# A decoder block on one core: chunk steps issued behind products, operands formed from PSUM, norm weights spread by matmuls

## The chip, the cores and the metric

The kernel runs on one core of a Trainium2 chip. The metric is the device time of one execution in microseconds, as a median over runs. TensorE (PE) multiplies, VectorE (DVE), ScalarE (ACT) and GpSimd (POOL) do the rest, and SyncE (SP) and ACT issue the DMAs. PSUM is the memory in which products arrive, SBUF the one for operands.

## The reference

One block of a hybrid decoder, all in float32: 1024 positions, model width 1024.

```python
u = rmsnorm(h, norm_mix_w)
gate_a, gate_s, b_a, c_a, v_a, z, xbc, dt_raw = split(u @ w_in)
y_a = (b_a * causal_dwconv(c_a * v_a, conv_a_w)) @ w_a_out        # short gated conv
xbc = silu(causal_dwconv(xbc, ssd_conv_w) + ssd_conv_b)           # width 4
y   = ssd_chunked_scan(xh, dt, a, bs, cs)    # 32 heads of 64, 4 groups, state 128, chunks of 128
y_s = gated_group_rmsnorm(y + d_skip * xh, z, ssd_norm_w) @ w_s_out
h   = h + (sigmoid(gate_a) * y_a + sigmoid(gate_s) * y_s) @ w_o
v   = rmsnorm(h, norm_ffn_w)
h   = h + conv_gated_mlp(v, w_up, ffn_conv_w, ffn_conv_b, w_down) # inner width 2816
return rmsnorm(h, final_norm_w)
```

Within a chunk of 128 positions the scan is a masked product with decays exp(a_cum[l] - a_cum[s]); between chunks a state per head is carried on.

## The kernel before, in words

Positions and inner dimensions are held as 128 partitions by 512 or 1024 columns. Every float32 product is made of three products of rounded parts: a value is split into hi (a cast on ACT, `split`, L148) and lo = value - hi (a subtraction on DVE or POOL, L149), and `product` (L268) adds hi x hi, hi x lo and lo x hi, 12 matmuls of 128x512 into one PSUM buffer.

The projections u @ W_in and v @ W_up use a scheme of the Strassen-Winograd kind: for two column blocks of weights and the two halves of positions and of the inner dimension, seven products take the place of eight. The operands of the activations are a11, a12 (first half of the positions, the two halves of the inner dimension), a22, s1, s2, s3, s4 (with a21 and a22 of the second half: s1 = a21 + a22, s2 = s1 - a11, s3 = a11 - a21, s4 = a12 - s2); those of the weights are b11, b21, b22 and the sums t1 to t4, which `Pair.operands` forms on POOL. `Pair` makes the seven products of a pair; sums so far (`m1`, `u2`, `u3`) are copied from PSUM by ACT (L311, L331) or added by DVE (L314, L333), and `done` hands a finished pair on. `then` interleaves the last products of a pair with the first of the next.

`rms_rows` (L174 to L179) normalises a tile of 128 positions: a square with its sum on ACT, a power on POOL, and one DVE instruction that multiplies by the row's factor and by the weights nw (L179), broadcast to all partitions by a DMA of 512 KB (L433, behind the first two x tiles). `fill_first` (L207) transposes a normalised tile of the first half on TensorE (`pt_u`), splits it into a11 and a12, and copies both from PSUM back over the tile. `fill_second` (L215) does the second half in three stages: s1 and a22 with an ACT copy of each PSUM tile (L233, L236), then s2 and s3 by DVE from those SBUF copies (L240, L242), then s4. For u the kept first half gives a11 and a12; for v, the FFN's input, POOL adds hi and lo again (L229). In names, u or v marks the operand: us4l is the lo part of u's s4.

The order: x is normalised and transposed; three gate pairs (`head`, names with g) start with their a11 and a12 products while the second half's operands are made; then come the dt columns, whose result `decays` turns into decays per head and position (a chain on DVE and ACT; 6 transposes `tkp`, L593, copied to the tile tk); then the pairs of BEFORE (xb: the conv's inputs, z) and BESIDE. From BESIDE on, a clock counts the products: after each, `tick` (L394) runs what is due. Each of 32 chunks (4 groups of 8) is a generator `ssd_chunk` whose stages are due at 17 + 6s + offset: LOAD_M and LOAD_IN -9 (DMAs on ACT's queue, L715, L718), DECAY -6 (8 relus and an exponential on ACT, L724, L725, to the mask tile m), TRANS -4 (transposes px, pb, product pc, L730 to L734; DVE multiplies m by pc, L752), LOAD_Z -3, DIAG 0 (products pd, po, pst, L770 to L783), SQUARES 3, NORM 6 (a column sum pn, L813, a power on POOL, L819, and each fourth chunk a transpose pr, L823). `conv4` (L604 to L617) makes four taps, a silu and the store of an xb tile.

Then follow the output products (`y_a`, `s_out`, `out_proj`), in whose shadow v is normalised (`v_norm`, L1000 to L1009) and v's operands filled, the up pairs (`ffn_pair`) and the down products.

A scheduler puts the instructions of each engine in order, from the order of the code and a model of their times; `tc.issue_after(i)` makes what is written in its block and runs on i's engine stand behind i. PSUM has four buffers for products (`mm`) and four for the rest (`sd`); c2 is a pool of 6 tiles of 512 columns, t2 one such tile.

Of the kernel before, what the change touches and what calls it, by code (L numbers as in the profile page):

```python
# [65 lines left out]
def tile_block(  # L66
# [147 lines left out]
    def fill_second(A, v, t, name, first=None, own=None):  # L214
# [8 lines left out]
        def whole(c, nm):  # L223

            if first is not None:
                return blocks(first[:, halves[c == "a12"]])
            hi, lo = (f32(a[:, :, ts]) for a in A[c])
            o = blocks(c2(f"{nm}{name}{t}"))
            pool.tensor_tensor(o, hi, lo, op=ALU.add)  # L229
            return o  # L230
# [2 lines left out]
        act.copy(s1, pts[1])  # L233
        dve.tensor_tensor(s1, s1, pts[0], op=ALU.add)
# [5 lines left out]
        dve.tensor_tensor(s1, s1, a11, op=ALU.subtract)  # L240
# [1 line left out]
        dve.tensor_tensor(a21, a11, a21, op=ALU.subtract)  # L242
# [3 lines left out]
        a12 = whole("a12", "a12")
        s4 = a12 if own is None else blocks(
            own.tile([P, HALF], F32, tag="own", name=f"own{name}{t}", bufs=4)
        )
        dve.tensor_tensor(s4, a12, s1, op=ALU.subtract)  # L250
        if first is not None:
# [9 lines left out]
    def product(ps, c, w, start=True, stop=True, held=False):  # L261


        hi, lo = (t.rearrange("p (k c) -> p k c", k=4) for t in w)
        n = 0
        for wt, ct in ((hi, c[0]), (hi, c[1]), (lo, c[0])):
            for k in range(4):
                pe.matmul(  # L268
                    ps, wt[:, k, :], ct[:, k, :],
                    start=(start and n == 0), stop=(stop and n == 11), skip_group_check=held,  # L270
                )
                n += 1

    class Pair:
# [27 lines left out]
        def first(self, late=False, hold=True, place=None):  # L302
# [8 lines left out]
            act.copy(self.m1, p)  # L311
# [16 lines left out]
        def so_far(self, o, c, w, nm):  # L328

            if self.hold:  # L330
                act.copy(o, self.prod(c, w, nm, self.u))  # L331
            else:
                dve.tensor_tensor(o, self.m1, self.prod(c, w, nm), op=ALU.add)  # L333
# [278 lines left out]
    def conv4(ci, t):  # L612
        cv = b4(f"cv{t}")
        taps(cv, ci, scw[:, t, :], scb[:, t : t + 1])
        act.activation(cv, cv, AF.Silu)
# [86 lines left out]
    def ssd_chunk(s):  # L702
# [116 lines left out]
        pool.tensor_tensor(r[:, c % 4 : c % 4 + 1], rs, nhalf, op=ALU.pow)  # L819
# [538 lines left out]
```

## Time and profile before

| | |
|---|---|
| median of 3 runs | 1973.09 us (1970.45 to 1977.09) |
| the profiled execution | 1974.46 us; its span 1972.7 us |
| busy: TensorE, DVE, ACT, POOL | 1914.5, 1289.6, 962.0, 1236.3 us |
| mean granted clock of TensorE | 0.989 of full speed |
| DMA | 338.42 MB, mean 172 GB/s |

The span is the time between the first and the last instruction of the profiled execution; 1.8 us lie around it. Busy time of one engine overlaps that of the others. The granted clock is the share of full speed that the throttle allows TensorE; a matmul under half the clock is busy for twice the time. A row of a group has the line in the kernel, engine, operation, output<-inputs, shape, count, then busy time and mean ns of one, then idle time of the engine ahead of it and what ended most of that. A row of a wait has the engine that waits, output and line of the waiting instruction, the releaser with its line, then total, count and longest.

### The profile page before, as it was taken

How to read it: one execution, taken by the hardware profiler on the slowest of the kernel's cores; microseconds unless marked ns; L12 is line 12 of the kernel's file. 1: busy time of each engine (PE TensorE's matmuls, PEld its weight loads, DVE VectorE, ACT ScalarE, POOL GpSimd, SP SyncE). 2: the span in 40 equal slices, each digit the busy share in tenths (PEclk: the TensorE clock that was granted, in tenths of full speed). 3: DMA queues.
4: the chain of work that ended last, by engine and by line, in shares of the span. 5: the costliest groups of instructions: out<-in, count | busy, mean ns of one | idle time of the engine just before them, and what ended most of it. 6: DMA issues, size and time to landing. Idle time of an engine off the chain costs nothing.

```text
span 1972.7 us, 25409 instructions
## 1 busy us (share of the span) xinstructions
PE 1914.5 (97%) x8986; PEld 1572.0 (80%) x8986; DVE 1289.6 (65%) x1429; ACT 962.0 (49%) x1636; POOL 1236.3 (63%) x915
## 2 busy tenths in 40 slices
PE   7899999999999999999999999998999999999998
PEld 6678887787788778888888888876888888878886
DVE  8655567767776777777664833479854655585555
ACT  6345457677546664443542323354344444453334
POOL 6657776866776776676445533458876787845342
PEclk9899999999999999999999999998999999999999
DMA  4133355545445554443998974451323344487653
GB/s 166 54 111 121 122 164 172 162 150 190 155 133 164 164 164 124 146 157 110 382 376 279 356 250 161 161 170 35 136 80 108 101 150 163 139 285 264 206 188 143
DMA packets 180175, 338.42 MB, mean 172 GB/s; under 512 B 15280, under 2 KB 87760, under 8 KB 179024
## 3 DMA queue, kind: packets, MB, share of 16 engines
q1 hardware_dynamic: 93264, 253.95, 37.7%
q10 hardware_dynamic: 86784, 82.85, 13.1%
q8 instruction: 70, 1.15, 0.2%
q14 instruction: 57, 0.47, 0.1%
HBM read 247.34 MB, written 89.41 MB: 171 GB/s over the span
## 4 chain that ended last, share of the span: by engine, by line
PE 80%; DVE 7%; ACT 4%; issue 3%; DMA 3%; POOL 2%; ACTq 1%; SPq 0%; POOLq 0%; DVEq 0%
PE pb11up L268 10%; PE so L268 9%; PE pt1up L268 6%; PE pb11xb L268 5%; PE ya L268 4%; PE pb11cv L268 4%; PE d L1151 3%; PE d L1153 3%; PE d L1152 3%; PE pb11z L268 3%; PE pb21up L268 3%; PE pb11ba L268 2%; PE pt1cv L268 2%; PE pt1xb L268 2%; DMA m<-acd 2%
## 5 line engine op out<-in xcount | busy, mean ns | idle before, releaser
L608 DVE SCALAR_TENSOR_TENSOR cv<-xbc,scw,cv 128x1024 f32<-128x1024 f32 x72 | 122.6, 1704 | 46.3 <-ACT cv L604 45.0
L608 DVE SCALAR_TENSOR_TENSOR h<-fci,fcw,h 128x1024 f32<-128x1024 f32 x44 | 85.9, 1953 | 74.1 <-ACT h L604 73.3
L724 ACT ACTIVATE m<-m,tk 128x128 f32<-128x128 f32 x256 | 79.1, 390 | 95.3 <-DMA m<-acd 91.4
L149 POOL TENSOR_TENSOR l_ws<-raw_ws,h_ws 128x512 fp32r<-128x512 f32 x32 | 46.3, 1447 | 71.1 <-PE so L268 40.8
L148 ACT CAST h_ws<-raw_ws 128x512 fp32r<-128x512 f32 x64 | 39.9, 623 | 96.8 <-PE so L268 69.3
L268 PE MATMUL so<-yh,h_ws 128*128 128x512 f32 x256 | 69.0, 391 | 0.0
L268 PE MATMUL so<-yl,h_ws 128*128 128x512 f32 x256 | 68.6, 389 | 0.0
L268 PE MATMUL so<-yh,l_ws 128*128 128x512 f32 x256 | 68.5, 389 | 0.0
L148 ACT CAST h_wo<-raw_wo 128x512 fp32r<-128x512 f32 x48 | 29.7, 621 | 60.3 <-PE wo L985 32.7
L808 DVE TENSOR_TENSOR eb<-eb 128x256 f32<-128x256 f32 x32 | 28.1, 879 | 45.6 <-ACT eb L806 45.6
L149 DVE TENSOR_TENSOR l_ws<-raw_ws,h_ws 128x512 fp32r<-128x512 f32 x32 | 25.1, 785 | 50.0 <-PE so L268 25.5
L149 POOL TENSOR_TENSOR l_wo<-raw_wo,h_wo 128x512 fp32r<-128x512 f32 x24 | 32.3, 1346 | 39.1 <-PE wo L985 30.7
L268 PEld LDWEIGHTS so<-yh,l_ws 128*128 128x128 f32 x256 | 48.0, 188 | 10.0
L268 PEld LDWEIGHTS so<-yl,h_ws 128*128 128x128 f32 x256 | 48.0, 188 | 10.0
L268 PEld LDWEIGHTS so<-yh,h_ws 128*128 128x128 f32 x256 | 47.8, 188 | 9.7
L1128 DVE TENSOR_TENSOR h<-h 128x1024 f32<-128x1024 f32 x22 | 48.7, 2212 | 9.8 <-ACT h L1127 9.6
L314 DVE TENSOR_TENSOR fci<-fci,pb21up 128x512 f32<-128x512 f32 x18 | 12.4, 688 | 60.3 <-PE pb21up L268 60.3
L149 POOL TENSOR_TENSOR l_t3up<-raw_2up,h_t3up 128x512 fp32r<-128x512 f32 x22 | 30.3, 1376 | 32.7 <-PE pb11up L268 32.7
L984 PE MATMUL wo<-l_wo,mh 128*128 128x512 f32 x128 | 50.0, 391 | 0.0
L983 PE MATMUL wo<-h_wo,mh 128*128 128x512 f32 x128 | 49.9, 391 | 0.0
L985 PE MATMUL wo<-h_wo,ml 128*128 128x512 f32 x128 | 49.7, 391 | 0.0
L1127 ACT ACTIVATE h<-h 128x1024 f32<-128x1024 f32 x22 | 23.4, 1062 | 52.7 <-DVE h L608 52.7
(1125 smaller groups left out, 6571.8 us busy)
## 6 DMA issues: line engine op xcount, KB each, us to landing
m<-acd ACTq DMA_DIRECT2D x32, 512.0 KB, 3.9
raw_ws<-in_w_s_out SPq DMA_DIRECT2D x32, 512.0 KB, 4.7
ssd_in<-cv ACTq DMA_DIRECT2D x24, 512.0 KB, 3.1
in<-ssd_in ACTq DMA_DIRECT2D x32, 384.0 KB, 3.8
raw_wo<-in_w_o SPq DMA_DIRECT2D x24, 512.0 KB, 3.8
wd<-in_w_down SPq DMA_DIRECT2D x22, 512.0 KB, 7.0
td<-wd SPq DMA_DIRECT2D x44, 256.0 KB, 4.3
raw_2up<-in_w_up SPq DMA_DIRECT2D x22, 512.0 KB, 3.4
```

Source lines behind the costliest of these rows:

```text
L148: act.copy(hi, v)
L149: (eng or pool).tensor_tensor(lo, v, f32(hi), op=ALU.subtract)
L268: pe.matmul(ps, wt[:, k, :], ct[:, k, :], start=(start and n == 0), stop=(stop and n == 11), skip_group_check=held,)
L608: dve.scalar_tensor_tensor(cv, ci[:, j : j + SEQ], w[:, j : j + 1], cv, op0=ALU.mult, op1=ALU.add)
L724: act.activation(m[:, h, :], m[:, h, :], AF.Relu, bias=a)
L983: pe.matmul(pss[t], mh, wh, start=k == 0, stop=False)
L984: pe.matmul(pss[t], mh, wl, start=False, stop=False)
L985: pe.matmul(pss[t], ml, wh, start=False, stop=k == NK - 1)
L1128: dve.tensor_tensor(cv, cv, h3, op=ALU.mult)
L1151: pe.matmul(ps, aa[0][:, ts], bb[0], start=k == 0, stop=False)
L1152: pe.matmul(ps, aa[0][:, ts], bb[1], start=False, stop=False)
L1153: pe.matmul(ps, aa[1][:, ts], bb[0], start=False, stop=k == KF - 1)
```

## The change

1. The norm weights nw come as one row of 4 KB (first on SP's queue); two f32 matmuls against a row of ones spread it over the partitions, and DVE copies it from PSUM.
2. `fill_first`: for u the lo part of a12 is made by POOL from the kept copy, and the kept copy of a11 by DVE instead of ACT. For v, a11 is now kept too (4 more ACT copies, a pool of its own).
3. `fill_second`: s3 and s2 are formed by DVE with one operand in PSUM; the ACT copy of a21 (8 of them) and POOL's new sum of a11 for v (4) are gone. For u, s4's split is a fourth stage, run within the first gate pair, behind the addition u2 of that pair on DVE.
4. The second gate pair's t2 gets a c2 buffer.
5. `decays` stops ahead of its transposes; these are written behind the third pair of BEFORE.
6. `tick`: what is due is issued behind the last matmul of the product (on TensorE) and behind the last copy of product sums (on ACT). conv4's silu and store come two products later. The transpose pr is a stage of its own, due at +8.

Instructions in all: PE 8528 to 8530, ACT 1838 to 1826, DVE 1431 to 1433, POOL and SP as before.

```diff
-STAGES = LOAD_M, LOAD_IN, DECAY, TRANS, LOAD_Z, DIAG, SQUARES, NORM = -9, -9, -6, -4, -3, 0, 3, 6
+STAGES = LOAD_M, LOAD_IN, DECAY, TRANS, LOAD_Z, DIAG, SQUARES, NORM, ROW = -9, -9, -6, -4, -3, 0, 3, 6, 8
...
-    def fill_first(A, v, t, name, keep=False):
+    def fill_first(A, v, t, name, keep=()):
 
         ts = slice(t * P, (t + 1) * P)
-        for pt, c, h in zip(transposed(v, name), ("a11", "a12"), halves):
-            split(pt, A[c][0][:, :, ts], A[c][1][:, :, ts], dve)
-            if keep:
-                act.copy(blocks(v[:, h]), pt)
+        for n, (pt, c) in enumerate(zip(transposed(v, name), ("a11", "a12"))):
+            hi, lo = (a[:, :, ts] for a in A[c])
+            act.copy(hi, pt)
+            if n < len(keep) and n:
+                act.copy(keep[n], pt)
+                pool.tensor_tensor(lo, keep[n], f32(hi), op=ALU.subtract)
+            else:
+                dve.tensor_tensor(lo, pt, f32(hi), op=ALU.subtract)
+                if n < len(keep):
+                    (dve.tensor_copy if len(keep) == 2 else act.copy)(keep[n], pt)
...
-        s1, a21 = (blocks(v[:, h]) for h in halves)
+        s1, s3 = (blocks(v[:, h]) for h in halves)
         act.copy(s1, pts[1])
         dve.tensor_tensor(s1, s1, pts[0], op=ALU.add)
         put("s1", s1)
-        act.copy(a21, pts[0])
         put("a22", pts[1])
+
+        dve.tensor_tensor(s3, a11, pts[0], op=ALU.subtract)
+        s2 = a11
+        dve.tensor_tensor(s2, pts[1], s3, op=ALU.subtract)
         yield
-        a11 = whole("a11", "a11")
-        dve.tensor_tensor(s1, s1, a11, op=ALU.subtract)
-        put("s2", s1)
-        dve.tensor_tensor(a21, a11, a21, op=ALU.subtract)
-        if first is None:
-            put("s3", a21, pool)
+        put("s2", s2)
+        if own is None:
+            put("s3", s3, pool)
             yield
...
+            dve.tensor_tensor(s4, a12, s2, op=ALU.subtract)
             yield
-            put("s3", a21, pool)
+            put("s3", s3, pool)
+            yield
         put("s4", s4)
         yield
...
-                pe.matmul(
+                mark["pe"] = pe.matmul(
...
-            act.copy(self.m1, p)
+            mark["act"] = act.copy(self.m1, p).ins
...
-                act.copy(o, self.prod(c, w, nm, self.u))
+                mark["act"] = act.copy(o, self.prod(c, w, nm, self.u)).ins
             else:
-                dve.tensor_tensor(o, self.m1, self.prod(c, w, nm), op=ALU.add)
-                self.m1 = o
+                i = dve.tensor_tensor(o, self.m1, self.prod(c, w, nm), op=ALU.add)
+                mark["dve"], self.m1 = i.ins, o
...
     def tick():
+
         if clock[0] is not None:
             clock[0] += 1
-            for f in slots.pop(clock[0], ()):
-                f()
+            with tc.issue_after(mark["pe"]), tc.issue_after(mark["act"]):
+                for f in slots.pop(clock[0], ()):
+                    f()
...
     nw = s4("nw_mix")[:, :DM]
+    for n, h in enumerate(halves):
+        pw = mm_tile(f"nw{n}")
+        pe.matmul(pw, ones[:1, :], nwr[:, h], start=True, stop=True)
+        dve.tensor_copy(nw[:, h], pw)
...
-            if t + i == NWAT:
-                sp.dma_start(nw, norm_mix_w.unsqueeze(0).to_broadcast([P, DM]))
...
-    for p in head[:2]:
-        p.operands()
+    for i, p in enumerate(head[:2]):
+        p.operands((t2, c2)[i])
...
-        act.activation(cv, cv, AF.Silu)
         g, slot = ssd_slot(t)
-        act.dma_start(xd_[g][:, slot, :], cv)
+
+        def end():
+            act.activation(cv, cv, AF.Silu)
+            act.dma_start(xd_[g][:, slot, :], cv)
+
+        later(2, end)
...
-        then(p)
+        if i == 0:
+            last[0] = p
+            p.s2()
+            with tc.issue_after(mark["dve"]):
+                stage(fills)
+            p.s3()
+        else:
+            then(p)
...
-    decays(dt_ps)
-    rows_.close()
-    ssp = mixer.enter_context(tc.tile_pool(name="ssp", bufs=1))
+    dec = decays(dt_ps)
+    next(dec)
...
         pool.tensor_tensor(r[:, c % 4 : c % 4 + 1], rs, nhalf, op=ALU.pow)
+        yield
         if c % 4 == 3:
...
-    for item in BEFORE:
+    for n, item in enumerate(BEFORE):
         run(*item)
+        if n == 2:
+            with tc.issue_after(mark["pe"]):
+                next(dec)
+    rows_.close()
+    ssp = mixer.enter_context(tc.tile_pool(name="ssp", bufs=1))
...
-            fill_first(V, v_norm(j // 2), j // 2, f"v{j // 2}")
+            fill_first(V, v_norm(j // 2), j // 2, f"v{j // 2}", v11[j // 2 : j // 2 + 1])
...
-        return fill_second(V, v, t - 4, "v")
+        return fill_second(V, v, t - 4, "v", v11[t - 4])
```

How the order of instructions moves is shown at three places. The first is ACT in the SSD stretch, where chunk m_4 is prepared (L715 loads it, L724 is its relus, L311 and L331 copy sums of products, L617 stores a convolved tile). Before:

```order
L311 COPY xbc_2625<-pb11xb_2631 128x512
L148 CAST h_b11g_2878<-raw_1g_2875 128x512
L615 ACTIVATE cv_2582<-cv_2582 128x1024
L715 DMA m_4_2774<-acd 128x1024
L617 DMA ssd_in_85<-cv_2582 128x1024
L724 ACTIVATE m_4_2774<-m_4_2774,tk 128x128 x8
```

After, on the same engine (the lines are those of the changed kernel: L749 is the load, L758 the relus, L331 the copy of sums, L660 and L661 silu and store of a z tile):

```order
L749 DMA m_4_2777<-acd 128x1024
L752 DMA in_4_2779<-ssd_in_84 128x6x128
L331 COPY u2xb_2750<-pb11xb_2634 128x512
L660 ACTIVATE z_2408<-z_2408 128x1024
L146 CAST h_t4xb_2942<-raw_1xb_2632 128x512
L661 DMA ssd_in_85<-z_2408 128x1024
L758 ACTIVATE m_4_2777<-m_4_2777,tk 128x128 x8
```

The load had one row between itself and the relus; now there are five, a copy of product sums among them.

The second place is DVE in the head, at u2g, the sum that the second gate pair's t2 product waits for. Before:

```order
L149 TENSOR_TENSOR us2l<-x_130,us2h 128x4x128
L149 TENSOR_TENSOR l_b22g_738<-raw_2g_548,h_b22g_737 128x512
L149 TENSOR_TENSOR us4l<-ownu_618,us4h 128x4x128
L149 TENSOR_TENSOR us4l<-ownu_624,us4h 128x4x128
L149 TENSOR_TENSOR us4l<-ownu_630,us4h 128x4x128
L149 TENSOR_TENSOR us4l<-ownu_636,us4h 128x4x128
L333 TENSOR_TENSOR u2g_677<-m1g_414,pt2g_678 128x512
```

After:

```order
L147 TENSOR_TENSOR us2l<-x_133,us2h 128x4x128
L314 TENSOR_TENSOR gt_521<-m1g_541,pb21g_543 128x512
L147 TENSOR_TENSOR l_b22g_741<-raw_2g_561,h_b22g_740 128x512
L333 TENSOR_TENSOR u2g_672<-m1g_425,pt2g_673 128x512
L147 TENSOR_TENSOR us4l<-ownu_629,us4h 128x4x128
L147 TENSOR_TENSOR us4l<-ownu_633,us4h 128x4x128
```

The four us4l stood ahead of u2g and now stand behind it.

The third place is DVE in the V stage, behind the last normalisation (L1009, after it L1046). Before, with L240 and L242 subtracting in SBUF (h is the tile, a11v POOL's sum):

```order
L1009 SCALAR_TENSOR_TENSOR h_11112<-h_11112,r_v_11575,nw_ffn 128x1024
L149 TENSOR_TENSOR l_t1up_11818<-raw_1up_11580,h_t1up_11817 128x512
L314 TENSOR_TENSOR fci_11619<-m1up_11640,pb21up_11642 128x512
L234 TENSOR_TENSOR h_11112<-h_11112,pt_v_11660 128x512
L240 TENSOR_TENSOR h_11110<-h_11110,a11v_11784 128x512
L242 TENSOR_TENSOR h_11110<-a11v_11784,h_11110 128x512
L149 TENSOR_TENSOR va22l<-pt_v_11665,va22h 128x4x128
L240 TENSOR_TENSOR h_11110<-h_11110,a11v_11792 128x512
```

After, with L236 forming s3 and L238 forming s2 from PSUM (pt_v) and the kept a11 (v_):

```order
L1046 SCALAR_TENSOR_TENSOR h_11126<-h_11126,r_v_11591,nw_ffn 128x1024
L147 TENSOR_TENSOR l_t1up_11820<-raw_1up_11596,h_t1up_11819 128x512
L314 TENSOR_TENSOR fci_11635<-m1up_11656,pb21up_11658 128x512
L247 TENSOR_TENSOR a12v_11870<-a12v_11870,v_10388 128x512
L232 TENSOR_TENSOR h_11126<-h_11126,pt_v_11676 128x512
L236 TENSOR_TENSOR h_11126<-v_10390,pt_v_11676 128x512
L147 TENSOR_TENSOR va22l<-pt_v_11681,va22h 128x4x128
L247 TENSOR_TENSOR a12v_11875<-a12v_11875,v_10389 128x512
```

The subtractions of two tiles moved ahead of the last normalisation, and those that stay have an operand in PSUM.

More of the change, by code (lines that the diff above doesn't have):

```diff
@@ L221, in put @@
             split(val, A[c][0][:, :, ts], A[c][1][:, :, ts], eng)
[L223 to L230, printed above, removed]
-        s1, a21 = (blocks(v[:, h]) for h in halves)
+        s1, s3 = (blocks(v[:, h]) for h in halves)
         act.copy(s1, pts[1])
@@ L235, in fill_second @@
         put("s1", s1)
-        act.copy(a21, pts[0])
         put("a22", pts[1])
+        dve.tensor_tensor(s3, a11, pts[0], op=ALU.subtract)
+        s2 = a11
+        dve.tensor_tensor(s2, pts[1], s3, op=ALU.subtract)
         yield
-        a11 = whole("a11", "a11")
-        dve.tensor_tensor(s1, s1, a11, op=ALU.subtract)
-        put("s2", s1)
-        dve.tensor_tensor(a21, a11, a21, op=ALU.subtract)
-        if first is None:
-            put("s3", a21, pool)
-            yield
[L246 to L251, printed above, removed]
+        put("s2", s2)
+        if own is None:
+            put("s3", s3, pool)
+            yield
+            s4 = blocks(c2(f"a12{name}{t}"))
+            hi, lo = (f32(a[:, :, ts]) for a in A["a12"])
+            pool.tensor_tensor(s4, hi, lo, op=ALU.add)
+            dve.tensor_tensor(s4, s4, s2, op=ALU.subtract)
+        else:
+            s4 = blocks(own.tile([P, HALF], F32, tag="own", name=f"own{name}{t}", bufs=4))
+            dve.tensor_tensor(s4, a12, s2, op=ALU.subtract)
             yield
-            put("s3", a21, pool)
+            put("s3", s3, pool)
+            yield
         put("s4", s4)
@@ L316, in first, with operands @@
                 self.operands()
-        def operands(self):
+        def operands(self, place=t2):
             name = self.name
@@ L321, in operands @@
             (b11, b21), (b12, b22) = ([r[:, h] for h in halves] for r in (r1, r2))
-            self.t1, self.t2, self.t3, self.t4, self.b22 = b11, t2(f"t2{name}"), b12, b21, b22
+            self.t1, self.t2, self.t3, self.t4, self.b22 = b11, place(f"t2{name}"), b12, b21, b22
             pool.tensor_tensor(self.t1, b12, b11, op=ALU.subtract)
@@ L396, in tick, with at, later @@
             clock[0] += 1
-            for f in slots.pop(clock[0], ()):
-                f()
+            with tc.issue_after(mark["pe"]), tc.issue_after(mark["act"]):
+                for f in slots.pop(clock[0], ()):
+                    f()
+    def at(n, f):
+        slots.setdefault(n, []).append(f)
+    def later(n, f):
+        if clock[0] is None:
+            f()
+        else:
+            at(clock[0] + n, f)
     xd_ = [dram.tile([P, 10, SEQ], F32, name=f"ssd_in{g}") for g in range(NG)]
@@ L424, in tile_block @@
     dve.memset(zeros, 0.0)
+    ones = const([P, P], "ones")
+    dve.memset(ones, 1.0)
+    nwr = wp.tile([P, 1024], F32, tag="raw", name="nw_row", bufs=NRAW)[:1, :DM]
+    sp.dma_start(nwr, norm_mix_w.unsqueeze(0))
     nw = s4("nw_mix")[:, :DM]
+    for n, h in enumerate(halves):
+        pw = mm_tile(f"nw{n}")
+        pe.matmul(pw, ones[:1, :], nwr[:, h], start=True, stop=True)
+        dve.tensor_copy(nw[:, h], pw)
     xs = []
@@ L437, in u_norm, with kept @@
         rms_rows(xs[t], nw, f"x{t}", xs[t], s4(f"sq{t}")[:, :DM])
+    def kept(v):
+        return [blocks(v[:, h]) for h in halves]
     for t in range(4):
         u_norm(t)
-        fill_first(U, xs[t], t, f"u{t}", True)
+        fill_first(U, xs[t], t, f"u{t}", kept(xs[t]))
     rows_ = ExitStack()
@@ L499, in tile_block @@
         u_norm(t)
-    fills = [fill_second(U, xs[t], t - 4, "u", xs[t - 4], cur["row"]) for t in range(4, 8)]
+    fills = [fill_second(U, xs[t], t - 4, "u", *kept(xs[t - 4]), cur["row"]) for t in range(4, 8)]
     stage(fills[:2])
@@ L683, in tile_block @@
         p.done = lambda p=p, i=i: gates_done((p.d1, p.d2), gad, 2 * i)
-        then(p)
+        if i == 0:
[4 more added lines that the diff above has]
+            p.s3()
+        else:
+            then(p)
     dt_add(dt1, "s1", (2, 3))
@@ L1034, in fill_beside @@
         if j % 2 == 0:
-            fill_first(V, v_norm(j // 2), j // 2, f"v{j // 2}")
+            fill_first(V, v_norm(j // 2), j // 2, f"v{j // 2}", v11[j // 2 : j // 2 + 1])
     V = operand("v")
+    kept_ = ExitStack()
+    kp = kept_.enter_context(tc.tile_pool(name="kp", bufs=1))
+    v11 = [blocks(kp.tile([P, HALF], F32, name=f"v11{t}")) for t in range(4)]
     mg = s_out(1, ys1, fill_beside)
```

14 lines of the change are left out of this document (7 added, 7 removed).

## The prediction

> **What bounds the kernel now.** I read the page first, then the stretches, then TensorE's waits in each stretch, last single instructions. The page:
>
> ```profile
> span 1972.7 us, 25409 instructions
> PE 1914.5 (97%) x8986; PEld 1572.0 (80%) x8986; DVE 1289.6 (65%) x1429; ACT 962.0 (49%) x1636; POOL 1236.3 (63%) x915
> PE 80%; DVE 7%; ACT 4%; issue 3%; DMA 3%; POOL 2%; ACTq 1%; SPq 0%; POOLq 0%; DVEq 0%
> ```
>
> TensorE is busy for 97% of the span, and the change takes no product from it. So two things can be won: its idle time (58.2 us over the span), and the time in which it works under a lower granted clock. The first line of the chain of waits gives DVE 7% and ACT 4%: those two hold TensorE up, wherever they do. The stretches (length, then busy time of PE, PEld, DVE, ACT, POOL, granted clock, DMA share, GB/s) tell where:
>
> ```profile
> 0.00:28.00 28.00, 15.58 (x84) 13.94 (x85) 19.96 (x40) 20.05 (x41) 10.38 (x20) 0.88 0.81 290
> 28.00:80.00 52.00, 44.65 (x201) 36.06 (x200) 45.85 (x47) 26.19 (x49) 41.92 (x29) 0.90 0.05 18
> 80.00:175.00 95.00, 89.77 (x400) 73.49 (x399) 48.07 (x61) 46.67 (x82) 54.05 (x43) 0.98 0.35 117
> 300.00:900.00 600.00, 587.18 (x3070) 477.46 (x3069) 451.71 (x536) 353.09 (x667) 421.69 (x321) 1.00 0.49 155
> 1300.00:1420.00 120.00, 109.13 (x470) 89.27 (x469) 107.18 (x102) 54.13 (x94) 94.77 (x63) 0.94 0.27 91
> ```
>
> The most that each can give is idle time plus busy time times the missing clock: start 12.4+1.9 = 14.3; head 7.4+4.5 = 11.8; decays and first pairs 5.2+1.8 = 7.0; SSD beside the products 12.8; the FFN norm and its operands ("V stage") 10.9+6.5 = 17.4. In the head and the V stage DVE is busy 45.85 of 52 and 107.18 of 120: there it is nearly the bound.
>
> **The start: norm weights.** The broadcast of 512 KB gives way to a row of 4 KB, sent before the x tiles, two matmuls against ones and two DVE copies.
>
> ```profile
> 8.77 2.48 DVE L179 SCALAR_TENSOR_TENSOR x<-x,r_x,nw_mix 128x1024 f32<-128x1024 f32 x2 [1.58 <-DMA nw_mix<-in_norm_mix_w]
> L179 DVE SCALAR_TENSOR_TENSOR x<-x,r_x,nw_mix x8: 1276/1280/2304, 8.8 to 27.2; 128x1024 f32<-128x1024 f32 x8
> L783 PE MATMUL pst<-xe,bk x56: 590/592/697, 272.6 to 895.1; 128*128 128x512 f32 x56
> PE pt_u L187 <- DVE x L179: 10.6, 2, 10.1
> ```
>
> The first normalisation waited 1.58 us for the weights; TensorE, with nothing else to do, waited for it. The added matmuls are f32 of 512 columns: by L783 0.6 us each, 1.2 together, on an idle engine, while x is still landing and squared. I take the 1.58 as won, -1.5; a little more is possible because x no longer shares the queue with 512 KB (to -2.5). Against it: POOL now makes four low parts (ua12l) beside the normalisations, and a disturbed normalisation takes 2.304 instead of 1.276; were four more of them disturbed, 4 x 1.03 = +4.1. That is the upper end. The lower end lies nearer, since the wait for the weights is certain and the splits come one at a time.
>
> The Trainium skill ("SBUF — State Buffer", Who interferes with whom) says that a DVE instruction with two SBUF inputs and a GpSimd instruction that reads SBUF lock each other out, while one with at most one SBUF input goes on. It speaks against the moved splits here (the +4.1), and for the PSUM operands below; the rows of the next part agree with it.
>
> **The head: second operands.** TensorE's waits from 28 to 175 us (total, count, longest), then DVE's groups from 28 to 75:
>
> ```profile
> PE pt2g L268 <- DVE u2g L333: 3.9, 1, 3.9
> PE pb11xb L268 <- ACT u3xb L331: 2.3, 1, 2.3
> PE tkp L593 <- DVE ee L559: 2.0, 1, 2.0
> PE pt2g L268 <- DVE us2l L149: 1.9, 1, 1.9
> PE pt1g L268 <- DVE us1l L149: 1.0, 1, 1.0
> PE pb11z L268 <- ACT u3z L331: 1.0, 1, 1.0
> L149 DVE TENSOR_TENSOR us4l<-ownu,us4h 128x512 fp32r<-128x512 f32 x4 | 6.8, 1760 | 3.7 <-POOL us3l L149 3.7
> L240 DVE TENSOR_TENSOR x<-x,x 128x512 f32<-128x512 f32 x4 | 5.4, 1353 | 0.0
> L242 DVE TENSOR_TENSOR x<-x,x 128x512 f32<-128x512 f32 x4 | 4.9, 1229 | 0.0
> L234 DVE TENSOR_TENSOR x<-x,pt_u 128x512 f32<-128x512 f32 x4 | 2.7, 680 | 0.6 <-ACT x L233 0.6
> 73.53 0.67 DVE L333 TENSOR_TENSOR u2g<-m1g,pt2g 128x512 f32<-128x512 f32 x1
> 74.26 2.07 PE L268 MATMUL pt2g<-us2h,h_t2g 128*128 128x512 f32 x4 [3.92 <-DVE u2g L333]
> ```
>
> The subtractions L240 and L242, both operands in SBUF, take 1.353 and 1.229 us; L234, with one in PSUM, 0.680. Made from PSUM, s3 and s2 cost 0.68 each: 4 x (2.58 - 1.36) = 4.9 us less on DVE ahead of s2's low parts, and four ACT copies (L236) fall away. Next, u2g, 0.67 us of work, stands on DVE behind four us4l of 1.76; the second pair's t2 product needs u2g's buffer of sums and waited 3.92. Now u2g stands ahead of them, and between u2g and the first product of s4 lie two others (s3, a22), so the cover for the late us4l (4 x 1.76 = 7.0 us) is two products of some 3.2 us, 12 matmuls each, and whatever else the scheduler puts between; if that cover is short, a wait of about 1 us at s4 is next. The second t2 in a buffer of its own (c2) lets POOL form it without waiting for the first.
>
> So of the waits for DVE, 3.9+1.9 = 5.8 go; us1l (1.0) stays, since nothing ahead of it is shortened. After a wait of 3.92 four matmuls took 2.07 us, half the clock; of the 4.5 us that the clock costs I take half, 2.2. Sum -8; bounds 0 (DVE's other work, 45.85 less 4.9, still ends as late) and -11.8.
>
> The Trainium skill ("TensorE: Matmul & The Clock Gate", Part 1) says the clock falls to half after an idle window of about 3.4 us and returns after as long a busy one; the trace agrees, 3.92 of idling before the slow group. By that rule all of the 4.5 comes back once no wait passes 3.4, and the term would be -10.
>
> **Decays.** The six transposes of tk (tkp) stood on TensorE's queue between products and waited 2.0 us for the exponentials' DVE work; now they stand behind the third pair, still ahead of their first user, the first chunk's relus. That 2.0 goes. The u3xb and u3z waits (2.3, 1.0) are ACT's: its copy of sums stood behind the first chunk's relus and their load. I take half of them, 1.6. Sum -3.5, bounds 0 (the later relus are late in turn) and -7.0.
>
> **SSD steps behind products and copies.** TensorE's waits from 300 to 900, the two of ACT that stand behind them, the mask product and the load:
>
> ```profile
> PE pb11xb L268 <- ACT u2xb L331: 2.9, 2, 1.6
> PE pr L823 <- POOL yr L819: 2.8, 3, 2.3
> PE pb11cv L268 <- ACT u2cv L331: 2.2, 1, 2.2
> PE pt1g L268 <- DVE gt L346: 1.5, 1, 1.5
> PE pb11cv L268 <- ACT cc L311: 1.2, 1, 1.2
> PE pb11xb L268 <- ACT u3xb L331: 1.0, 1, 1.0
> PE pn L813 <- DVE ss L810: 0.7, 1, 0.7
> ACT m L724 <- DMA m<-acd: 78.4, 21, 6.9
> ACT cv L615 <- DVE cv L608: 19.1, 8, 5.8
> L752 DVE TENSOR_TENSOR m<-m,cb x32: 1209/1227/2318, 268.3 to 904.3; 128x1024 f32<-128x1024 f32 x32
> ```
>
> ACT sat 78.4 us on the relus' load, 21 times, because the load is issued one to five instructions ahead; and 19.1 on the conv's silu. When a copy of product sums stands behind such a wait, its PSUM buffer comes free late and the next product waits: 2.9+2.2+1.2+1.0 = 7.3 us here. In the new order one to three such copies stand between load and relus, and the silu comes two products later, so most of these ACT waits shrink below what the products notice. I take two thirds, 4.9. The row transposes (pr) move two products behind POOL's power: 2.8 goes. The waits for DVE (gt, ss) stay. For new ones (a group of chunk matmuls now stands whole between products, and its first waits for all) I set 2 against it, the size of the largest single wait above. Sum -6 (5.7 rounded); bounds +2 and -12.8. The DMAs of the moved steps, 24 of ssd_in, 32 of m and 32 of in, go with them on ACT's queue; their issue now stands behind the copies. The store of a convolved tile goes two products later as well; its reader, the load of a chunk's input, is asked for nine products ahead of the chunk, and I count nothing for it; were that cover gone, the chunk's first matmuls would wait, which is inside the +2.
>
> **V stage.** TensorE's waits from 1300 to 1400 and DVE's groups from 1314 to 1372:
>
> ```profile
> PE pt_v L187 <- DVE h L1009: 3.9, 1, 3.9
> PE pt1up L268 <- DVE vs1l L149: 3.9, 1, 3.9
> PE pt2up L268 <- DVE vs2l L149: 3.1, 1, 3.1
> L240 DVE TENSOR_TENSOR h<-h,a11v 128x512 f32<-128x512 f32 x4 | 6.3, 1564 | 0.0
> L242 DVE TENSOR_TENSOR h<-a11v,h 128x512 f32<-128x512 f32 x4 | 6.0, 1496 | 0.0
> ```
>
> Here each tile saves 1.564+1.496-2x0.680 = 1.70 us, 6.8 for four, and DVE no longer waits for POOL's a11 sums. The kept a11 adds four ACT copies in the first half; ACT is busy 54.13 of 120, so nothing waits for them. Of the 7.0 that products waited for vs1l and vs2l I take 6 (the 6.8, less what splits of weights queue in between), and a third of the clock's 6.5, 2.2; the norm's own 3.9 stays. Sum -8, bounds 0 and -17.4.
>
> **The sum.** -1.5-8-3.5-6-8 = -27. The profiled execution took 1974.46, its span 1972.7: 1974.46-27 = 1947.5. The median of the runs, 1973.09, is 1.4 lower: 1946. A time within 0.3% (5.9 us) cannot be told from no change.
>
> **Rivals.**
> Order without effect: ACT's idle time is moved, not shortened, since silu, table loads and DMA issues still come ahead of the copies; the 19.1 of silu waits speak for it, the 78.4 against. SSD and decays give nothing but pr and tkp (-4.8): 1946+4.7 = 1951.
> DVE stays the bound: in head and V it is over 88% busy, and what is saved ahead of u2g comes back behind it. Half of both terms: 1954.
> Port at the start: POOL's splits disturb the normalisations, +4.1 instead of -1.5: 1952. This is what the Trainium skill's SBUF page (Who interferes with whom) would have.
> Full recovery: both bound stages run without waits over 3 us, and -38 or beyond: 1935 to 1928.
> Nothing: new waits eat it all, 1967 to 1979.
> Slower: the relus and the exponential now stand one to three products later, 3 to 10 us, while the diagonal product (pd) keeps its place, so m x cb on DVE may be late for it. It decides once the mask product is later than the three products that still lie between exponential and pd, some 10 us. One such product's 1.227 at each of 32 chunks: 39 us, 1985. Against it: DVE is busy 451.71 of 600 there, so its queue is rarely so long.
>
> **How the numbers follow.** The sum as it stands, 1937 to 1956 with its terms' errors: 0.48. No effect of the order 0.13, DVE bound 0.13, port 0.05, full recovery 0.08, nothing 0.07, slower 0.06. The first five lie below 1967.2: faster 0.87, same 0.07, slower 0.06. The range goes from 1928, where all but 0.04 of the full recovery is inside, to 1966, where nothing and slower are left out: 0.17 outside.
>
> **What would show it.** Start: the first normalisation at about 7 us with no DMA named. Head: clock of the stretch above 0.95, u2g ahead of us4l, no wait of 3.9 at pt2g. Decays: no wait at tkp. SSD: ACT's wait for m below 30 us in the same 600, and no copy named ahead of pb11. V: subtractions near 0.7 us and waits for vs1l and vs2l under 1. Wrong it is if pd waits for m, if the normalisations rise to 2.3, or if the FFN norm's tiles come later than before, since two of their low parts now stand ahead of a tile's norm on DVE.

## The result and the profile after

The changed kernel takes 1954.16 us (median of 4 runs, 1953.78 to 1954.97) against 1972.94 us before: a ratio of 0.9904 (95% interval 0.9892 to 0.9917), 18.8 us less. The forecast was 1946, range 1928 to 1966. The profiled execution took 1953.78 us.

The head of the page of the changed kernel:

```profile
span 1952.0 us, 25330 instructions
PE 1908.6 (98%) x8990; PEld 1568.4 (80%) x8990; DVE 1287.3 (66%) x1431; ACT 951.7 (49%) x1624; POOL 1233.9 (63%) x915
PE 79%; ACT 5%; issue 5%; DVE 4%; DMA 3%; POOL 3%; ACTq 1%; SPq 0%; POOLq 0%; DVEq 0%
```

Its stretches, with the bounds and columns of before:

```profile
28.00:80.00 52.00, 47.05 (x222) 38.33 (x221) 45.13 (x52) 23.61 (x44) 43.18 (x30) 1.00 0.10 36
80.00:175.00 95.00, 95.00 (x435) 79.09 (x434) 58.73 (x63) 46.72 (x73) 67.75 (x49) 1.00 0.34 113
300.00:900.00 600.00, 583.58 (x3036) 475.98 (x3035) 446.59 (x530) 341.06 (x659) 420.74 (x321) 0.99 0.49 153
1300.00:1420.00 120.00, 114.94 (x502) 93.09 (x501) 98.73 (x100) 54.99 (x92) 100.97 (x68) 0.99 0.26 93
```

The idle time of the decay stretch is gone, the clock is whole in the head, and the V stage has half of its idle time left. But from 300 to 900 TensorE is busy for less than before, 583.58 of 600 in place of 587.18.

Since the bounds of a stretch cut the two kernels at different products, the shares of the 20.7 us are better read from where the same products stand. Start times on TensorE, from the two traces:

| product | before | after | shift | gained since the row above |
|---|---|---|---|---|
| first gate product (pb11g) | 29.4 | 27.8 | -1.6 | 1.6 |
| last pt2g of the head | 93.3 | 85.2 | -8.1 | 6.5 |
| first chunk's px | 259.8 | 244.1 | -15.7 | 7.6 |
| last product of ba (pb11ba) | 923.4 | 912.6 | -10.8 | -4.9 |
| last s_out product (so) | 1268.4 | 1257.6 | -10.8 | 0 |
| last pt1up | 1762.3 | 1741.5 | -20.8 | 10.0 |

Four stretches give 25.7 us, and the stretch with the chunks takes 4.9 of it back: 663.6 us before, 668.5 after. TensorE's waits there (300 to 905; total, count, longest), of the changed kernel:

```profile
PE pb21g L268 <- DVE yss L849: 3.2, 2, 2.0
PE pn L847 <- DVE ss L844: 2.5, 1, 2.5
PE pc L768 <- DVE eb L820: 2.3, 1, 2.3
PE pt1g L268 <- DVE gt L346: 1.9, 2, 1.7
PE pd L804 <- DVE m L786: 1.8, 1, 1.8
PE pb11xb L268 <- ACT xbc L311: 1.4, 1, 1.4
PE pr L858 <- POOL yr L853: 1.1, 1, 1.1
PE pb L766 <- DVE eb L820: 0.8, 1, 0.8
PE pb11cv L268 <- ACT u3cv L331: 0.8, 1, 0.8
PE pc L768 <- DVE st L827: 0.3, 1, 0.3
```

Before, 7.7 us of this were waits for ACT and 2.2 for DVE; now 2.2 are for ACT and 12.8 for DVE. The waits of ACT and DVE themselves in the changed kernel (245 to 905):

```profile
ACT m L758 <- DMA m<-acd: 19.5, 13, 3.7
DVE l_b22xb L147 <- ACT h_b22xb L146: 32.6, 5, 9.6
```

and the row of the same cast before:

```profile
DVE l_b22xb L149 <- ACT h_b22xb L148: 4.7, 4, 2.2
```

ACT's wait for the load fell as forecast. What was not forecast: ACT now issues the cast h_b22xb, which a product's weights need, behind chunk work, and DVE, which splits those weights, stands at l_b22xb for up to 9.6 us. One such place, on ACT, DVE and TensorE in turn (start, duration):

```profile
456.72 0.59 ACT L331 COPY u2xb<-pb11xb 128x512 f32<-128x512 f32 x1 [2.17 <-PE pt1z L268]
...
462.47 2.45 ACT L758 ACTIVATE m<-m,tk 128x128 f32<-128x128 f32 x8 [3.70 <-DMA m<-acd]
464.82 0.60 ACT L146 CAST h_t2g<-t2g 128x512 fp32r<-128x512 f32 x1
465.33 1.06 ACT L660 ACTIVATE z<-z 128x1024 f32<-128x1024 f32 x1
466.41 1.28 ACT L759 ACT_TABLE_LOAD   x1
467.70 1.06 ACT L759 ACTIVATE m<-m 128x1024 f32<-128x1024 f32 x1
468.67 0.60 ACT L146 CAST h_b22xb<-raw_2xb 128x512 fp32r<-128x512 f32 x1
...
459.07 0.68 DVE L363 TENSOR_TENSOR z<-u2z,pt1z 128x512 f32<-128x512 f32 x1
469.30 0.69 DVE L147 TENSOR_TENSOR l_b22xb<-raw_2xb,h_b22xb 128x512 fp32r<-128x512 f32 x1 [9.55 <-ACT h_b22xb L146]
469.91 0.15 DVE L849 TENSOR_SCALAR yss<-pn 128x1 f32<-128x1 f32 x1
...
470.11 1.20 PE L268 MATMUL pb21g<-ua12h,h_b21g 128*128 128x512 f32 x4 [2.01 <-DVE yss L849]
```

The chain reads from bottom to top: the product b21 needs an sd buffer of PSUM; one still holds the column sum pn, read by yss; yss takes 0.15 us but stands on DVE behind l_b22xb; and that waits for a cast that ACT has behind the relus, a silu, a table load and the exponential.

### The profile page after: what moved, and what is told of

It is laid out like the page before. It is cut to its first block, busy times and chain, and to the rows that moved or that the text cites. A ratio compares the mean times of both kernels' runs of the same rounds, so it can differ in the third digit from the quotient of the medians.

```text
span 1952.0 us, 25330 instructions
## 1 busy us (share of the span) xinstructions
PE 1908.6 (98%) x8990; PEld 1568.4 (80%) x8990; DVE 1287.3 (66%) x1431; ACT 951.7 (49%) x1624; POOL 1233.9 (63%) x915
## 4 chain that ended last, share of the span: by engine, by line
PE 79%; ACT 5%; issue 5%; DVE 4%; DMA 3%; POOL 3%; ACTq 1%; SPq 0%; POOLq 0%; DVEq 0%
PE pb11up L268 9%; PE so L268 9%; PE pb11xb L268 5%; PE pt1up L268 5%; PE ya L268 5%; PE pb11cv L268 4%; PE d L1193 3%; PE d L1194 3%; PE d L1192 3%; PE pb11z L268 3%; PE pb21up L268 2%; PE pt1xb L268 2%; PE pb11g L268 2%; PE pb11ba L268 2%; PE pt1cv L268 2%
## 5 line engine op out<-in xcount | busy, mean ns | idle before, releaser
L630 DVE SCALAR_TENSOR_TENSOR h<-fci,fcw,h 128x1024 f32<-128x1024 f32 x44 | 85.2, 1937 | 74.0 <-ACT h L626 73.4
L758 ACT ACTIVATE m<-m,tk 128x128 f32<-128x128 f32 x256 | 78.4, 390 | 19.5 <-DMA m<-acd 19.5
L786 DVE TENSOR_TENSOR m<-m,cb 128x1024 f32<-128x1024 f32 x32 | 57.6, 1801 | 0.2
L147 POOL TENSOR_TENSOR l_wo<-raw_wo,h_wo 128x512 fp32r<-128x512 f32 x24 | 32.9, 1373 | 36.7 <-PE wo L1022 30.7
L147 POOL TENSOR_TENSOR l_t3up<-raw_2up,h_t3up 128x512 fp32r<-128x512 f32 x22 | 30.7, 1397 | 32.2 <-PE pb11up L268 32.2
L853 POOL TENSOR_TENSOR yr<-yss,nhalf 128x1 f32<-128x1 f32 x32 | 23.5, 735 | 42.9 <-DVE yss L849 36.7
```

What stands on the lines that cost most here:

```text
L147: (eng or pool).tensor_tensor(lo, v, f32(hi), op=ALU.subtract)
L630: dve.scalar_tensor_tensor(cv, ci[:, j : j + SEQ], w[:, j : j + 1], cv, op0=ALU.mult, op1=ALU.add)
L758: act.activation(m[:, h, :], m[:, h, :], AF.Relu, bias=a)
L786: dve.tensor_tensor(m, m, cb.unsqueeze(1).to_broadcast([P, HG, P]), op=ALU.mult)
```

## The experiments

Each is the changed kernel with one edit; medians of 4 runs or more beside runs of the kernel before on the same chip. "Chunk stretch" is the time from the first px to the last pb11ba in the kernel's own trace.

| kernel | median us | ratio to before (95%) | chunk stretch | waits of TensorE for ACT, DVE, 300 to 905 |
|---|---|---|---|---|
| before | 1972.94 | | 663.6 | 7.7, 2.2 |
| changed | 1954.16 | 0.9904 (0.9892 to 0.9917) | 668.5 | 2.2, 12.8 |
| s_plain: no marks | 1941.24 | 0.9838 (0.9822 to 0.9855) | 661.1 | 8.9, 1.3 |
| s_pe: TensorE's mark alone | 1940.77 | 0.9837 (0.9822 to 0.9851) | 657.9 | 6.9, 0 |
| s_act: ACT's mark alone | 1952.67 | 0.9895 (0.9881 to 0.9910) | 666.4 | 1.3, 9.4 |
| t_decay: ACT's mark for the decay stage | 1944.93 | 0.9862 (0.9847 to 0.9877) | 660.1 | 0.7, 8.8 |
| t_dsq: decays and squares | 1947.43 | 0.9876 (0.9854 to 0.9897) | 662.7 | 0.6, 9.4 |
| t_dload: decays and loads | 1943.88 | 0.9856 (0.9836 to 0.9876) | 658.6 | 1.0, 8.1 |
| t_dcopy: all but loads and squares | 1944.35 | 0.9859 (0.9839 to 0.9880) | 661.3 | 1.2, 9.2 |
| t_nodecay: all but the decays | 1967.0 | 0.9977 (0.9965 to 0.9989) | 682.2 | 6.0, 12.9 |

Stretches and waits come from one trace each. The traced runs of s_plain and v_sum lie 3.9 and 3.0 us above their medians, the others within 2.3; and five traces with all marks in place (the changed kernel, d_early, us4_old, s23_sbuf and v_sum) have chunk stretches from 666.0 to 668.5. So 2 or 3 us between two stretches say little. t_dsq, t_dload, t_dcopy and v_sum ran beside 1970.83 us for the kernel before, the other experiments beside 1972.9: across the two groups the ratios compare, not the medians.

**The two marks.** The edits, of `tick`:

```diff
-            with tc.issue_after(mark["pe"]), tc.issue_after(mark["act"]):
+            # s_plain: neither; s_act: mark["act"] alone; s_pe: mark["pe"] alone
```

> The changed kernel, with the chunk steps run after each product as before, issued behind nothing (conv4's later silu and the later row transpose stay). Theory A (the mark on TensorE makes a chunk's small matmuls stand as a block ahead of the next product, so their waits for DVE reach the products: 10 us of new waits from 300 to 905; the mark on ACT saves 5.5 of the 7.7 us of waits for ACT's copies): the 10 go, the 5.5 come back, 1954.2-10+5.5 = about 1950, and the waits of pb21g for yss, pc for eb and pd for m are gone. Theory B (DVE is late in this stretch whatever the marks do; the marks only saved ACT's waits): about 1960, waits for DVE still near 11 us, waits for ACT near 7.

> The changed kernel, with the mark on ACT's copies alone (none on TensorE). Theory A: the 5.5 us saved stay and most of the 10 us of new waits go: 1945 to 1949. Theory B: as the changed kernel, 1953 to 1956.

> The changed kernel, with the mark on TensorE's last matmul alone (none on ACT). Theory A: the new waits for DVE stay (about 10 us), the ACT waits come back (5.5): 1958 to 1961. Theory B: the same 1958 to 1961 from the ACT waits, but with the waits for DVE no larger than without the mark.

Both theories fell. Without marks the time is 13 us less, as A had it in sign, but it is not TensorE's mark that costs: with that alone the time is the same as with none (1940.77 and 1941.24, the ranges overlap) and the chunk stretch the shortest of all, 657.9. With ACT's mark alone nearly all of the loss is there, 666.4 and 1952.67. TensorE's waits with its mark alone, the same stretch:

```profile
PE pb11xb L268 <- ACT u2xb L331: 2.9, 2, 1.4
PE pr L858 <- POOL yr L853: 2.4, 1, 2.4
PE pb11cv L268 <- ACT cc L311: 1.9, 1, 1.9
```

The waits for ACT's copies are about what they were before (u2xb 2.9, cc 1.2), and none for DVE has come. In s_pe ACT does the cast at 458.25 and waits for the load only afterwards:

```profile
458.25 0.62 ACT L146 CAST h_b22xb<-raw_2xb 128x512 fp32r<-128x512 f32 x1
...
462.08 0.33 ACTq L749 DMA_DIRECT2D m<-acd  x1
467.23 0.40 ACT L758 ACTIVATE m<-m,tk 128x128 f32<-128x128 f32 x1 [5.19 <-DMA m<-acd]
```

So ACT's mark trades 4.7 us of waits for ACT (6.9 with TensorE's mark alone, 2.2 with both) for 12.8 us of waits for DVE (0 to 12.8). A part of the loss is clock. The chunk stretch of the changed kernel, by its columns as above:

```profile
244.10:912.60 668.50, 652.08 (x3401) 532.14 (x3400) 503.41 (x591) 386.31 (x737) 462.27 (x355) 0.99 0.49 154
```

and of s_pe:

```profile
244.30:902.20 657.90, 648.74 (x3401) 530.90 (x3400) 485.02 (x592) 385.38 (x728) 466.77 (x355) 1.00 0.49 156
```

For the same count of matmuls TensorE idles 16.4 us in the one and 9.2 in the other, and is busy 3.3 us longer at a granted clock of 0.99 in place of 1.00: 7.3 + 3.3 make up the 10.6. Of the 3.3, an estimated 1.7 are one more stretch of 3.4 us at half clock (its row is in the last section); the other 1.6 are not placed. s_plain keeps conv4's later silu and the later pr; against before, its stretch is 2.5 us shorter, the pr wait of 2.8 having gone.

DVE differs in one more way. For the same work it is busy 503.4 us in the stretch of the changed kernel and 485.0 in that of s_pe. The mask product of m and cb (shortest, median and longest in ns), of the changed kernel and then of s_pe:

```profile
L786 DVE TENSOR_TENSOR m<-m,cb x32: 1210/2032/2320, 254.7 to 894.1; 128x1024 f32<-128x1024 f32 x32
L786 DVE TENSOR_TENSOR m<-m,cb x32: 1208/1226/2320, 252.9 to 882.5; 128x1024 f32<-128x1024 f32 x32
```

By the timelines, 20 of the changed kernel's took over 1.5 us, and POOL was busy for 0.91 of their time; for the 12 shorter ones it was 0.13. s_pe has 10 long ones. So with ACT's mark more of DVE's work runs beside POOL's and takes longer. That is a rival, as the cause of DVE's lateness, to its wait for the cast, and no run separates the two. It does not set the time alone: t_dload has 499.9 us of DVE in a stretch of 658.6.

**What stands behind ACT's mark.** A slot's stage decides whether ACT's mark holds:

```diff
+            for o, f in slots.pop(clock[0], ()):
+                with tc.issue_after(mark["pe"]):
+                    if o != DECAY:        # t_nodecay; t_decay: o == DECAY
+                        with tc.issue_after(mark["act"]):
+                            f()
+                    else:
+                        f()
```

> The changed kernel, with the mark on ACT for every chunk stage and silu but the decay stage (8 relus and an exponential); the mark on TensorE for all. Theory C, formed after the three runs on marks (behind the mark the relus wait for their load ahead of the next weights' cast h_b22xb on ACT, DVE stands still in its queue at l_b22xb, and what a chunk's products wait for of DVE comes late): the wait of DVE for h_b22xb falls from 32.6 to under 12 us and the time to 1939 to 1945. Rival D (it is the number of things behind the mark, squares, copies, silus and DMAs alike): 1948 to 1954.

> The changed kernel, with the mark on ACT for the decay stage alone; the mark on TensorE for all. Theory C: nearly all of the loss stays, 1950 to 1956, DVE's wait for h_b22xb over 20 us. Rival D: 1941 to 1946.

Theory C fell: with the decay stage alone behind the mark, 1944.93, nearly all of the loss is gone, though DVE's wait for the cast is not:

```profile
DVE l_b22xb L147 <- ACT h_b22xb L146: 27.5, 5, 8.7
```

(245 to 905, of t_decay.) The time is the one of rival D. TensorE's waits for DVE came with the decay stage, 8.8 us, but those for ACT fell from 6.9 to 0.7 and that of 2.4 for POOL went, so that the sum, 9.5, is about s_pe's 9.3. So DVE's stand at the cast is not enough by itself; that it costs only when what stands behind it on DVE (sums, pn's read) is already late is a reading that was not tested. t_nodecay cannot be read as the counterpart: at the place shown above, its ACT still has the relus (472.89) ahead of the cast (479.09), and DVE waits 39.0 us for h_b22xb, more than in the changed kernel. Why it is so slow (1967.0) stays open; ACT's 66.2 us of waits for loads do not explain it, since s_pe has 84.1.

> The changed kernel, with the mark on ACT for the decay and the squares stages alone (the mark on TensorE for all). With decays alone the time was 1944.9, with all stages 1954.2: 9 us lie in the others. Theory E (the squares: behind a copy they give DVE its sums late, the column sum pn waits for ss, and its PSUM buffer, read late, holds up pb21g): 1949 to 1954, with waits of pn for ss and of pb21g for yss over 4 us together. Rival F (the loads) and G (silus and small copies): 1943 to 1947.

> The changed kernel, with the mark on ACT for the decay stage and the three loads of a chunk alone. Theory F (a chunk's loads go out one or two products later, so what reads them is late, relus on ACT and the transposes and masks behind them): 1949 to 1954. Rivals E and G: 1943 to 1947.

> The changed kernel, with the mark on ACT for all but the loads and the squares (decay, small copies bk, st and rr; conv4's silu and store). Theory G (silu and store, and the small copies, stand ahead of casts): 1949 to 1954. Rivals E and F: 1943 to 1947. If the three runs each lie near 1947 the cost is no single stage's.

For t_dsq the condition is o in (DECAY, SQUARES), for t_dload o in (DECAY, LOAD_M, LOAD_Z), which takes in LOAD_IN, due at the same offset as LOAD_M, and for t_dcopy o not in (LOAD_M, LOAD_Z, SQUARES). By the chunk stretch, against 660.1 with the decays alone: squares +2.6, loads -1.5, small copies and silus +1.2. The intervals of the ratios overlap, and the stretches differ by about as much as traces with the same marks do, so neither settles these. The squares show their place, which theory E had named, a wait for the column sum (300 to 905, of t_dsq):

```profile
PE pn L851 <- DVE ss L848: 4.1, 1, 4.1
```

Added up, 657.9 + 2.2 + 2.6 - 1.5 + 1.2 = 662.4; all together measure 668.5. The missing 6 us appear only when the stages stand behind the mark together, so theories E, F and G each fall as the single cause (1947.43, 1943.88 and 1944.35, where each wanted 1949 or more); E's sign came, and the squares come nearest. That one block behind one copy grows too long for the casts is a reading that is left, with the timeline above as its example, and so is DVE's longer work; neither was tested further.

**The decays' transposes.**

```diff
     dec = decays(dt_ps)
     next(dec)
+    next(dec)
...
-        if n == 2:
-            with tc.issue_after(mark["pe"]):
-                next(dec)
```

> The changed kernel, with the six transposes of the decays back directly behind their chain. Theory A (the move itself saved the 2.0 us wait at tkp and the 3.3 us at u3xb and u3z, whose copies stood behind chunk steps): 1956 to 1960, with a wait at tkp of about 2. Rival (these waits went for another reason, such as the earlier second operands): 1953 to 1955, no wait at tkp.

1955.18 (ratio 0.9907, 0.9893 to 0.9922): the time does not show it, the trace does. The wait is back:

```profile
PE tkp L614 <- DVE ee L579: 2.1, 1, 2.1
```

and the first px starts at 248.5 instead of 244.1. The chunk stretch is 2.5 us shorter (666.0 instead of 668.5), which is no more than such traces differ by: us4_old enters it 5.3 us late and s23_sbuf 10.3, and theirs are 668.0 and 668.2. The u3xb and u3z waits did not come back, so they had gone for another reason, as the rival had it.

**u's s4 back ahead of u2g.**

```diff
     stage(fills)
     stage(fills)
+    stage(fills)
...
-        if i == 0:
-            last[0] = p
-            p.s2()
-            with tc.issue_after(mark["dve"]):
-                stage(fills)
-            p.s3()
-        else:
-            then(p)
+        then(p)
```

> The changed kernel, with the split of u's s4 back ahead of the first gate pair's t2 sums (u2g behind four us4l on DVE). Theory A, as predicted: the wait of 3.9 us at pt2g and a group at half clock come back, the head's last pt2g matmul starts 4 to 6 us later than 85.2, and the time is 1956 to 1960. Rival: the PSUM operands have already made DVE early enough: within 1 us, 1953 to 1955.

1958.05 (0.9928, 0.9913 to 0.9943), as expected, though the interval still meets that of the changed kernel (to 0.9917). The trace is plainer: the last pt2g starts at 90.5, 5.3 us later, the group behind the wait takes 2.08 us in place of 1.07, and the wait is the one of before:

```profile
PE pt2g L268 <- DVE u2g L333: 3.7, 1, 3.7
```

**s3 and s2 in SBUF.**

```diff
-        dve.tensor_tensor(s3, a11, pts[0], op=ALU.subtract)
-        s2 = a11
-        dve.tensor_tensor(s2, pts[1], s3, op=ALU.subtract)
+        act.copy(s3, pts[0])
         yield
+        s2 = s1
+        dve.tensor_tensor(s2, s1, a11, op=ALU.subtract)
+        dve.tensor_tensor(s3, a11, s3, op=ALU.subtract)
```

> The changed kernel, with s3 and s2 of both operands formed in SBUF from an ACT copy, as before (v's kept a11 stays, so POOL's sums are still gone). Theory A: DVE spends 2.6 to 3.0 us per tile instead of 1.4, the head's end is 3 to 5 us later and the V stage 4 to 7 us longer: 1960 to 1966. Rival (DVE's rest sets the end of both stages): 1953 to 1956.

1966.27 (0.9968, 0.9957 to 0.9979), just above the upper end. The head's last pt2g starts at 95.5, 10.3 us later than in the changed kernel and 2.2 later than before; from the last so to the last pt1up 6.9 us are gained in place of 10.0. In the V stage the waits are now at the norm (1280 to 1420), where the changed kernel has 1.0:

```profile
PE pt_v L185 <- DVE h L1047: 6.4, 2, 4.4
```

The head's 10.3 us are not the price of the subtractions alone. They hold a wait that neither the kernel before nor the changed one has (28 to 175), for the cast of an s1 that DVE formed late in this order:

```profile
PE pt1g L269 <- ACT us1h L146: 5.7, 1, 5.7
```

**v's a11 summed by POOL.**

```diff
-            fill_first(V, v_norm(j // 2), j // 2, f"v{j // 2}", v11[j // 2 : j // 2 + 1])
+            fill_first(V, v_norm(j // 2), j // 2, f"v{j // 2}")
...
+        if own is None:
+            hi, lo = (f32(a[:, :, ts]) for a in A["a11"])
+            pool.tensor_tensor(a11, hi, lo, op=ALU.add)
         dve.tensor_tensor(s3, a11, pts[0], op=ALU.subtract)
```

> The changed kernel, with v's a11 summed again by POOL from hi and lo (no ACT copy in the first half), s3 and s2 still from PSUM. With these in SBUF the V stage lost 3.1 of the 10.0 us that it had gained. Theory A (the rest is POOL's sums, which DVE waited for): 4 to 7 us longer, 1958 to 1961. Rival (the rest is the earlier order of the first two tiles' subtractions, and POOL's sums were hidden): within 2, 1953 to 1956.

1949.92 (0.9891, 0.9872 to 0.9910), not slower than the changed kernel's 0.9904; the stretch to the last pt1up gains 9.4 in place of 10.0, and the traces whose V stage is the changed kernel's gain 9.0 to 11.2. POOL's sums were hidden, the rival was right, and the four ACT copies bought nothing that shows.

A version that beats both kernels is among these: s_pe, the change without ACT's mark, 1940.77 us, 0.9837 of before.

## Why the prediction was right or wrong

| term | forecast | measured |
|---|---|---|
| start | -1.5 | -1.6 |
| head | -8 | -6.5 |
| decays and first pairs | -3.5 | -7.6 |
| chunks beside products | -6 | +4.9 |
| V stage | -8 | -10.0 |
| sum | -27 | -20.8 |

The time lies inside the range, but not because the sum was right. The chunk term missed by 10.9 us; start, decays and V stage gave 6.2 more than forecast and the head 1.5 less, and that the misses went against each other is luck. The rival "DVE stays the bound" names 1954, the time that came, but not for its reason: it halved head and V stage, which together gave 16.5 us where 16 were forecast.

**Start.** Right. The normalisation starts at 7.1 instead of 8.8, after a broadcast that now costs two DVE copies:

```profile
L177 DVE SCALAR_TENSOR_TENSOR x<-x,r_x,nw_mix x8: 1276/1772/2306, 7.1 to 31.4; 128x1024 f32<-128x1024 f32 x8
L446 DVE COPY nw_mix<-nw x2: 691/692/692, 4.4 to 6.1; 128x512 f32<-128x512 f32 x2
```

The port's rival was seen at work: the median of the eight normalisations rose from 1280 to 1772 ns with POOL's splits beside them, as the Trainium skill has it ("SBUF — State Buffer", Who interferes with whom). The longest took 2306 (2304 before). But the products did not wait for the longer normalisations: the first gate product came 1.6 us earlier. That weights and splits were not undone one by one leaves open how much each is worth.

**Head.** Right in its mechanism. u2g stands ahead of the four us4l, and us4_old shows that place worth 5.3 us; without the PSUM operands s23_sbuf loses 10.3, new wait and all. Each is its loss with the other in place, so they do not add up: all of the change gained 6.5 there. The clock came back whole (0.90 to 1.00), where the sum took half, and the 1.0 at us1l, which was to stay, went as well; but new waits, which the sum had left out, took their place:

```profile
PE pt3g L268 <- ACT gt L354: 2.1, 1, 2.1
PE pt3g L268 <- DVE u3g L333: 1.7, 1, 1.7
```

**Decays.** Undersized: all of the stretch's 7.0 came back, not half, and 0.6 more that I cannot place. The tkp wait went with the move (d_early brings it back); I had kept half of the u3xb and u3z waits as certain to be late again, and none was.

**Chunks.** This step failed. The trace's largest idle entry, ACT's 78.4 us for loads, was read as the cause of 7.3 us of product waits, and it fell as forecast, to 19.5; the product waits for ACT fell too, 7.7 to 2.2. What failed is the "2 set against it" for new waits: it was 10.6 (2.2 to 12.8 for DVE), and the term came out beyond its bound of +2. Of ACT's waits the sum expected most to shrink; the one for the conv's silu grew instead, from 19.1 to 30.7 us (300 to 900), and pr's wait fell to 1.1, not to nothing. I had asked whose copy stands behind the relus, but not which casts would stand behind them once they were moved, nor what waits behind those on DVE. Of the signs I named for this step, ACT's wait for m below 30 came true without the gain: it was a sign of the move, not of its worth. That no copy would be named ahead of pb11 came true but for two (1.4 and 0.8 us). The plainest answer is s_pe: its chunk stretch is 5.7 us shorter than before, the size that I forecast, while ACT waits 81.8 us for the loads from 300 to 900. So the size came without the move that I put it down to. The slower rival's place, pd for m, came at one chunk with 1.8 us; it was one of nine waits for DVE.

**V stage.** Right in size, partly for another reason. I let the norm's 3.9 stay and took 6 of the 7.0 at vs1l and vs2l. In the trace after (1280 to 1420):

```profile
PE pt1up L268 <- DVE vs1l L147: 2.7, 1, 2.7
PE pt_v L185 <- DVE h L1046: 1.0, 1, 1.0
PE pt2up L268 <- DVE u2up L333: 0.7, 1, 0.7
```

The norm's wait fell by 2.9, vs1l's by only 1.2 (it was to fall below 1), vs2l's went. The norm's tiles came earlier, the last at 1314.8 in place of 1328.0, so that sign of being wrong stayed away. The PSUM operands are worth 3.1 of the 10.0, POOL's sums 0.6, which is within the spread of the traces; the other 6 were not traced to one edit.

## What to carry to other kernels

An engine's long idle time is no price: ask which product waits behind it, and, before the idle instruction is moved, what will stand behind it at the new place, and who waits for that on the next engine's queue. When chunk work is tied to a place in the order, do not tie it on the engine that makes the casts: that cost 11 to 13 us here, while tying it on TensorE cost nothing and gained nothing clear of the noise. Put the operand that is already in PSUM into the subtraction; and read a term's worth from where the same product stands in both traces, since fixed bounds in time cut the two kernels at different products.

## What the runs showed of the hardware

After a wait of 2.75 us in the V stage of the changed kernel, four matmuls took 1.65 us (start, duration, wait) and the next four 1.91, against 1.07 in the rows at full clock; the granted clock was 0.50 from 1334.4 to 1336.0. In the head of the kernel before, a wait of 3.92 had been followed by a group of 2.07:

```profile
1332.77 1.65 PE L268 MATMUL pt1up<-vs1l,h_t1up 128*128 128x512 f32 x4 [2.75 <-DVE vs1l L147]
```

The Trainium skill ("TensorE: Matmul & The Clock Gate", Part 1) gives an idle window of about 3.4 us; here matmuls were slower after less. The chunk stretch shows it three times more. The changed kernel's runs at 1.00 but for two stretches of 3.4 us, which follow waits of 2.27 (pc for eb) and 2.48 us (pn for ss); s_pe's has one, after a wait of 1.88 (pb11cv for cc). In the columns of before, two rows of the changed kernel and one of s_pe:

```profile
497.00:500.40 3.40, 3.40 (x9) 2.61 (x9) 3.40 (x3) 0.00 (x0) 3.40 (x2) 0.50 0.35 142
698.40:701.80 3.40, 3.40 (x12) 2.36 (x10) 2.27 (x5) 2.96 (x5) 2.86 (x3) 0.50 0.31 128
502.20:505.60 3.40, 3.40 (x10) 2.63 (x8) 0.49 (x2) 2.12 (x3) 3.40 (x4) 0.51 0.40 158
```

Not every such wait costs that: the groups behind the 2.01 us at pb21g (470.11) took 1.20 and 1.08.
